# Hybrid trunk in FP32 parts: the first keys piece by half k, rotated 256-column pieces read in turn, boundary transposes in mid-unit

## The chip, the cores and the metric

One core of one Trainium2 chip runs the whole program. The metric is the time of one execution on the device in microseconds (us); the time before is a median of three runs.

## The reference

Two layers of a residual trunk over 256 tokens of width 1024. Each layer normalises the stream (RMS norm), multiplies it by one wide input matrix and feeds three parallel mixers: a Mamba-2 scan (A), sliding-window attention with rotated queries and keys (B) and forgetting attention (C). Their outputs are projected, gated, merged, projected once more and added to the stream; a last RMS norm ends it.

```python
for layer in range(DEPTH):
    h = rms_norm(x, norm_w[layer])
    proj = jnp.einsum('bsd,de->bse', h, w_in[layer])
    (a_xbc, a_z, a_dt, b_q, b_k, b_v, b_z, c_q, c_k, c_v, c_f, c_z, gates) = jnp.split(proj, split_at, axis=-1)
    y_a = mamba2_branch(a_xbc, a_z, a_dt, ...)
    y_b = sliding_window_branch(b_q, b_k, b_v, b_z, sinks[layer], cos, sin)   # rotates q and k
    y_c = forgetting_attention_branch(c_q, c_k, c_v, c_f, c_z, f_bias[layer])
    branch = jnp.einsum('bsiw,iwd->bsid', jnp.stack([y_a, y_b, y_c], axis=2), w_proj[layer])
    g = jax.nn.sigmoid(gates.reshape(b, s, N_BRANCH, d) + gate_bias[layer])
    x = x + jnp.einsum('bsd,de->bse', jnp.sum(g * branch, axis=2), w_out[layer])
return rms_norm(x, final_norm_w)
```

What matters here is the input product, the rotation (`rope`) of queries and keys, and the passage from one layer's output to the next layer's input.

## The kernel before

**Products.** The 256 tokens are two tiles of 128 (t = 0, 1), the width 1024 is eight steps k of 128 (`NK`). Every FP32 operand is split in two parts: a high part written by ScalarE in the matmul's format, and a low part, the difference, written by VectorE (`split`, line 255; the instructions carry lines 257 and 258). A product is three passes: high times high, low times high, high times low. `dense` (271) runs them for one tile and one weight piece k by k; `tok` (445) calls it with the tokens as the stationary operand and the weights moving. A unit is one piece for one tile: 24 matmuls.

**Weights.** A piece is 256 to 512 columns of a matrix. It is loaded on the SP queue in parts of up to 512 KB (`load_part`), six ahead (`N_RAW`), and split ahead as buffers come free (`feed`, `release`). A part of 256 columns holds four steps k.

**In turn.** With `turn` the moving operand is read in the order column 0, column n/2, column 1, and so on (`in_turn`, 237), and the result is put back in order where it leaves PSUM (`ordered`, 243). All pieces of 512 columns, the values piece of layer 0 and the pieces of the channel units are read so. Not so: the keys piece of layer 0, the queries 3 of both layers (256 columns) and the 272-column piece with the decay inputs and queries 0.

**Order.** `ops` (1067 to 1161) is a list of units by hand; TensorE takes them in that order. Work that hangs on a unit's result (transposes, attention, normalisation) waits in a list as a generator with a due time on a modelled TensorE clock (`launch`, with delays such as `D_H`), and `pump` puts what is due between units, or inside one where `tok` is given a `mid` (after the fourth k; by itself only for pieces of over 300 columns). `drain` forces it. The other engines' order follows from a scheduler, except in the opening, which is written out by hand.

**Opening (layer 0, lines 1193 to 1292).** x arrives in two loads for tile 0 and one for tile 1, among the first weight parts. `turn(t, j)` transposes half a tile on TensorE (four transposes) and multiplies by the norm weight on VectorE (1218); `high` (1222) and `low` (1226) split it; `w_high` (1230) and `w_low` (1234) split a weight part by halves, some of the lows on GpSimd (`gtt`). The row sums of squares come from `square` on ScalarE; the factor `y0.rn` is not yet known when the products run, so it multiplies their results later. The keys piece is the first: all passes of tile 0 with `second_rows` (the transposes of tile 1) behind its 16th and 20th matmul, then the splits of tile 1 (`first_end`), then tile 1. Its eviction waits in `late`. Then come the values piece, queries 1 and 2 (one piece of 512 columns), queries 3 (256), the 272-column piece, and `normalize`, which scales the transposed rows for everything after.

**Rotation.** `rope` (463) multiplies the result in PSUM by cosines and sines, three VectorE operations (472 without, 474 with the row factor), and GpSimd adds (498, 522).

**Boundary.** `out_end` (1003) adds the residual, takes the row factor of the finished stream, scales it (1037) and launches `hT` with `D_H[t]`, which transposes and splits a tile for the next layer. Layer 1 begins with keys and values tile 0, queries 3 tile 0, `drain(6)`, keys and values tile 1, queries 3 tile 1. `layer_consts` (400) loads a layer's small constants: for layer 0 on GpSimd's queue, for layer 1 on ScalarE's, listed late in layer 0.

Of the kernel before, what the change touches and what calls it, by code (L numbers as in the profile page):

```python
# [44 lines left out]
def hybrid_trunk(  # L45
# [149 lines left out]
        s.insert(axis, n)  # L195
        return ap.unsqueeze(axis).to_broadcast(s)

    def rsqrt(v, n):

        r0 = T("sm", [P, 8])  # L200
        nc.gpsimd.tensor_tensor(r0[:, :n], v[:, :n], mhalf[:, :n], op=ALU.pow)
        a = T("sm", [P, 8])
# [68 lines left out]
    def dense(pt, ah, al, bh, bl, w, after=None, mid=None):  # L271

        passes = ((ah, bh), (al, bh), (ah, bl))
        if after is None:
            seq = [(k, a, b) for k in range(NK) for a, b in passes]
        else:
            seq = [(k, a, b) for k0 in (0, 4) for a, b in passes for k in range(k0, k0 + 4)]
        for i, (k, a, b) in enumerate(seq):  # L280
            mm(pt, a(k), b(k), start=(i == 0), stop=(i == len(seq) - 1))
            if after is not None:
                after.get(i + 1, lambda: None)()
            elif i % 3 == 2:
                if w.last and (k + 1) % w.kper == 0:
                    release(w, k // w.kper + 1)
                if mid is not None and k == NK // 2 - 1:
                    mid()

    def dense2(ps_, as_, b, w, mids):  # L290

# [21 lines left out]
    late = []  # L313

    class Piece:
        def __init__(self, n):
# [128 lines left out]
    def tok(ah, al, w, t, turn=True, mid=None, bank=pmm, **kw):  # L445


        n = w.n
        p = bank()
        b = in_turn if turn else lambda ap: ap  # L450
        if mid is None and n > 300:
            mid = pump
        dense(p[:, 0:n], lambda k: ah[:, t, k, :], lambda k: al[:, t, k, :], lambda k: b(w.hi(k)),
              lambda k: b(w.lo(k)), w, mid=mid, **kw)
        return ordered(p[:, 0:n]) if turn else p[:, 0:n]

    def tok2(ah, al, w, mids):
# [4 lines left out]

    def rope(y, p, t):

        p4 = p.rearrange("p (h d) -> p h d", h=4)
        a = T("L1", [P, 4, 64])
        b = T("L1", [P, 4, 64])
        for o, i, r in ((a, p4, rope_sb[:, t, 0, :]),
                        (b[:, :, 0:32], p4[:, :, 32:64], rope_sb[:, t, 1, 0:32]),
                        (b[:, :, 32:64], p4[:, :, 0:32], rope_sb[:, t, 1, 32:64])):  # L470
            if y.rn is None:
                tt(o, i, bc(r, 1, 4), op=ALU.mult)
            else:
                stt(o, i, y.rn[:, t:t + 1], bc(r, 1, 4), op0=ALU.mult, op1=ALU.mult)
        return a, b

    def u_bkv(y, c0, t, after=None, end=lambda: None):

        def f(w):
            p = tok(y.hTh, y.hTl, w, t, turn=w.n == 512 or c0 > 0, after=after,  # L480
                    bank=pmx if after and t == 0 else pmm)
            end()
            if t == 0 and c0 == 0:
                kv = T("L8", [P, 2048])
                y.kT = kv[:, 0:1024].rearrange("p (h s) -> p h s", h=4)
                y.bv = kv[:, 1024:1536].rearrange("p (t c) -> p t c", t=2)
            (late.append if after is not None else lambda g: g())(lambda: evict(w, p))

        def evict(w, p):
            if c0 > 0:  # L490
                act(halves(y.bv[:, t, :]), p, AF.Copy, scale=y.rn[:, t:t + 1])
            elif w.n == 512:
                act(y.bv[:, t, :], p[:, 1, :], AF.Copy)
            if c0 == 0:
                a, b = rope(y, p if w.n == 256 else p[:, 0, :], t)
# [12 lines left out]
        return f  # L508

    def u_bq(y, c0, t):  # L510

        def f(w):
            p = tok(y.hTh, y.hTl, w, t, turn=w.n == 512)
            if w.n == 272:
                logits(y, t, 0, p[:, 0:16])
                p = p[:, 16:272]
            for i in range(w.n // 256):
                if t == 0:
                    y.qT[c0 + i] = T("qt", [P, 2, S])
                with tc.high_priority():  # L520
                    a, b = rope(y, p[:, i, :] if w.n == 512 else p, t)
# [545 lines left out]
    for y in layers:  # L1067
# [37 lines left out]

        if l == 0:
            k, v = cols(C_BK), cols(C_BV)
            op(k, u_bkv(y, 0, 0, {16: lambda: second_rows(0), 20: lambda: second_rows(1)}, lambda: first_end()))
            op(k, u_bkv(y, 0, 1, {}))
            op(v, u_bkv(y, 256, 0), u_bkv(y, 256, 1))  # L1110
# [82 lines left out]
    with tc.manual_schedule(engines={ENG.PE, ENG.DVE, ENG.Activation, ENG.Pool}):  # L1193
        load_to(2)
        nc.sync.dma_start(x0[:, 1, :], x2[P:S, :])
        nc.sync.dma_start(rope_sb, rope_tab.rearrange("(t p) c d -> p t c d", p=P))
        load_to(N_RAW)
        warm = pmx()
        for i in range(WARM):
# [29 lines left out]
            raw, hi, _ = part  # L1229
            act(hi[:, k:k + 2, :], raw[:, k:k + 2, :], AF.Copy)  # L1230

        def w_low(part, k, sub_=tt):
            raw, hi, lo = part
            sub_(lo[:, k:k + 2, :], raw[:, k:k + 2, :], hi[:, k:k + 2, :].bitcast(F32), op=ALU.subtract)

        def square(t, j):
            sum_sq(x0, t, 512 * j, ss[:, 2 * t + j:2 * t + j + 1], 512)

        parts = [new_part() for _ in range(4)]
        square(0, 0)  # L1240
        turn(0, 0)
        w_high(parts[0], 0)
# [15 lines left out]

        def second_rows(j):
            turn(1, j)  # L1260

        def first_end():
            high(1, 0)
            high(1, 1)
            low(1, 0)
            low(1, 1)
            w_high(parts[2], 0)
            w_high(parts[2], 2)
            w_low(parts[2], 2, gtt)
            w_low(parts[2], 0)  # L1270
            w_high(parts[3], 0)
            w_high(parts[3], 2)
            w_low(parts[3], 0)
            square(1, 0)
            square(1, 1)
            w_low(parts[3], 2)
            v = T("sm", [P, 8])
            nc.vector.tensor_reduce(v[:, 0:2], ss.rearrange("p (t j) -> p t j", t=2), axis=mybir.AxisListType.X,
                                    op=ALU.add)
            ts(v[:, 0:2], v[:, 0:2], 1.0 / D, EPS, op0=ALU.mult, op1=ALU.add)  # L1280
            y0.rn = rsqrt(v, 2)

        for i, f, _ in ops[:2]:
            f(pieces[i])
# [40 lines left out]
```

## Time and profile before

| | |
|---|---|
| runs without a profile | 841.45 us median, 841.16 to 841.69 |
| the profiled execution | 840.82 us, of it span 839.1 us |
| granted TensorE clock | 0.999 |
| TensorE busy | 830.2 us |
| VectorE, ScalarE, GpSimd busy | 650.0, 510.9, 108.1 us |
| loaded and stored | 157.85 MB, 188 GB/s in the mean |

The span runs from the first to the last instruction that the profile has; what lies around it (1.7 us) is not in any row. A row of the time line is start, length, engine, line, operation, result and sources with their sizes, count, and in brackets how long the engine was idle before and what ended that. PE is TensorE's matmuls, PEld its loads of the stationary operand, DVE VectorE, ACT ScalarE, POOL GpSimd, SP the queue of the loads; ACTq and POOLq are what those engines' sequencers do themselves. The matmul's recorded length includes its passage through the array, so the pace is read from start to start. In the chain of the work that ended last a piece is start, length and what it was; pieces with x24 are 24 matmuls in a row with nothing between. A row of the table of windows gives busy time and count of PE, PEld, DVE, ACT and POOL, the granted clock, the DMA engines' share and the GB/s moved.

### The profile page before, as it was taken

The numbers are of one execution on the slowest core, as the hardware profiler recorded it, in microseconds if no ns is written. First come the engines' busy times: TensorE is split into PE (matmuls) and PEld (weight loads), VectorE is DVE, ScalarE is ACT, GpSimd is POOL, SyncE is SP. The second block draws the span as 40 slices with busy tenths as digits, with TensorE's granted clock in tenths as the row PEclk, the third lists the DMA queues.
The fourth block names the chain that finished last, engine by engine and source line by source line (L and its number), as shares of the span: only waits on it lengthen the run. The fifth ranks groups of instructions, "written<-read, shape, count | busy, mean of one in ns | idle before, by whom it ended". The sixth has DMA issues, their size and how long they took to land.

```text
span 839.1 us, 16279 instructions
## 1 busy us (share of the span) xinstructions
PE 830.2 (99%) x6067; PEld 768.3 (92%) x6067; DVE 650.0 (77%) x1421; ACT 510.9 (61%) x1022; POOL 108.1 (13%) x144
## 2 busy tenths in 40 slices
PE   9999999999999999999999999999999999999996
PEld 8999999989999998888989999999899999988896
DVE  6897898998766679665777689899968667785665
ACT  7477768665666667353654676876557667654442
POOL 3810001000231010210024000100003110121000
PEclk9999999999999999999999999999999999999999
DMA  9755467666565556675676544766856564476622
GB/s 308 232 168 169 119 184 232 202 213 205 152 197 176 152 164 214 207 243 178 219 234 208 150 126 149 226 214 188 251 168 183 158 186 152 154 237 214 213 101 76
DMA packets 122841, 157.85 MB, mean 188 GB/s; under 512 B 5730, under 2 KB 89818, under 8 KB 122762
## 3 DMA queue, kind: packets, MB, share of 16 engines
q1 hardware_dynamic: 108816, 140.53, 53.4%
q10 hardware_dynamic: 13690, 16.24, 6.2%
q8 instruction: 48, 0.79, 0.4%
q14 instruction: 31, 0.25, 0.1%
q0 software_dynamic: 256, 0.05, 0.0%
HBM read 154.63 MB, written 2.16 MB: 187 GB/s over the span
## 4 chain that ended last, share of the span: by engine, by line
PE 99%; DVE 0%; ACT 0%; issue 0%; POOLq 0%; POOL 0%
PE mm L97 84%; PE mx L97 10%; PE mx L101 5%; DVE L L258 0%; DVE L L1218 0%; POOLq L1321 0%; ACT L L1031 0%; DVE L L1226 0%; ACT L L257 0%; DVE L L1006 0%; DVE L L1010 0%; POOL ident masks.py:199 0%; DVE sm L226 0%; POOL tri L168 0%; DVE sm L252 0%
## 5 line engine op out<-in xcount | busy, mean ns | idle before, releaser
L258 DVE TENSOR_TENSOR lo<-raw,hi 128x1024 fp32r<-128x1024 f32 (+3 forms) x262 | 310.6, 1199 | 89.6 <-ACT hi L257 81.6
L97 PE MATMUL mm<-hi,L 128*128 128x512 f32 (+4 forms) x1424 | 377.2, 352 | 0.7 <-ACT L L257 0.3
L257 ACT ACTIVATE hi<-raw 128x1024 fp32r<-128x1024 f32 (+3 forms) x262 | 264.1, 1022 | 90.1 <-PE mm L97 79.8
L97 PE MATMUL mm<-L,hi 128*128 128x256 f32 x1792 | 318.0, 278 | 0.0
L97 PEld LDWEIGHTS mm<-L,hi 128*128 128x128 f32 x1792 | 277.7, 192 | 7.4 <-issue 3.9
L97 PEld LDWEIGHTS mm<-hi,L 128*128 128x128 f32 x1424 | 251.0, 189 | 27.3 <-issue 2.1
L97 PE MATMUL mm<-lo,L 128*128 128x512 f32 (+4 forms) x712 | 247.2, 349 | 0.0
L97 PE MATMUL mm<-L,lo 128*128 128x256 f32 x896 | 246.4, 275 | 0.0
L97 PEld LDWEIGHTS mm<-L,lo 128*128 128x128 f32 x896 | 171.9, 192 | 0.2
L97 PEld LDWEIGHTS mm<-lo,L 128*128 128x128 f32 x712 | 134.3, 189 | 12.6 <-DVE lo L258 0.2
L877 POOL TENSOR_SCALAR_AFFINE_SELECT bias<-bias 128x128 f32<-128x128 f32 x64 | 35.8, 595 | 407.7 <-DMA bias<-cumd 211.8
L570 ACT ACTIVATE pp<-pp,nm 128x128 f32<-128x128 f32 (+1 forms) x128 | 56.6, 443 | 13.8 <-DVE nm L564 11.7
L699 DVE SCALAR_TENSOR_TENSOR L<-L,vec,L 128x255 f32<-128x255 f32 (+2 forms) x96 | 45.9, 479 | 2.1 <-ACT L L696 1.1
L702 ACT ACTIVATE L<-L 128x256 f32<-128x256 f32 x32 | 13.3, 417 | 41.1 <-DVE L L699 41.0
L97 PE MATMUL mx<-L,L 128*64 128x128 f32 (+1 forms) x384 | 34.4, 314 | 0.0
L901 ACT ACTIVATE L<-L 128x512 f32<-128x512 f32 x24 | 15.1, 630 | 31.1 <-DVE L L900 31.0
L582 DVE TENSOR_SCALAR pp<-pp,rsum 128x128 f32<-128x128 f32 (+1 forms) x128 | 32.3, 315 | 0.3
L97 PEld LDWEIGHTS mx<-L,L 128*64 128x64 f32 x384 | 23.0, 136 | 8.3 <-issue 1.4
L783 ACT ACTIVATE L<-mm 128x256 f32<-128x256 f32 x48 | 18.1, 378 | 20.2 <-PE mm L97 20.2
L599 ACT ACTIVATE L<-mx 128x512 f32<-128x512 f32 x48 | 26.8, 596 | 1.2 <-PE mx L101 1.0
L101 PE MATMUL mx<-ident,pp 128*128 128x128 f32 x192 | 26.3, 273 | 0.0
L900 DVE TENSOR_TENSOR L<-mm,L 128x512 f32<-128x512 f32 x24 | 16.4, 684 | 9.7 <-PE mm L97 9.7
(188 smaller groups left out, 731.8 us busy)
## 6 DMA issues: line engine op xcount, KB each, us to landing
raw<-in_w_in_dram SPq DMA_DIRECT2D x179, 512.0 KB, 4.4
raw<-in_w_proj_dram SPq DMA_DIRECT2D x48, 512.0 KB, 5.2
raw<-in_w_out_dram SPq DMA_DIRECT2D x16, 512.0 KB, 5.1
raw<-in_w_in_dram SPq DMA_DIRECT2D x16, 344.0 KB, 3.2
L<-cumd ACTq DMA_DIRECT2D x8, 512.0 KB, 4.7
bias<-cumd ACTq DMA_DIRECT2D x16, 256.0 KB, 3.4
L<-in_gate_bias_dram ACTq DMA_DIRECT2D x12, 256.0 KB, 6.3
raw<-in_w_in_dram SPq DMA_DIRECT2D x8, 352.0 KB, 3.1
```

What stands on the lines that cost most here:

```text
L97: nc.tensor.matmul(o, a, b, **kw)
L101: nc.tensor.transpose(o, a, i)
L257: keep(act)(hi, src, AF.Copy)
L258: keep(tt)(lo, src, hi.bitcast(F32), op=ALU.subtract)
L570: act(pp[:, i, sl], pp[:, i, sl], AF.Exp, scale=-1.0, bias=nm[:, e:e + 1], accum_out=sums[:, e:e + 1])
L582: ts(pp[:, i, sl], pp[:, i, sl], rs[:, 2 * i + b:2 * i + b + 1], 0.5, op0=ALU.mult, op1=ALU.mult)
L599: act(pT, pt, AF.Copy)
L699: stt(a[:, s:S], x_[:, 0:S - s], y.vec[:, 16 * j + u:16 * j + u + 1], a[:, s:S], op0=ALU.mult, op1=ALU.add)
L783: act(halves(th), p, AF.Tanh, scale=0.5)
L877: nc.gpsimd.affine_select(out=bias[:, i, dst], in_=bias[:, i, src], compare_op=ALU.is_ge, fill=NEG, base=0, pattern=[[-1, P]], channel_mul ...
L900: tt(halves(g), p, halves(y.gb), op=ALU.add)
L901: act(g, g, AF.Tanh, scale=0.5)
```

## The change

The keys piece of layer 0 is computed by half k for both tiles: a new function `keys` issues four matmuls, and the opening lists them by hand with the transposes of tile 1 between. All weight lows of the opening are on VectorE. The opening's end is written out in place of `second_rows` and `first_end`. The keys piece, and queries 3 in both layers, are read in turn (`turn=w.n != 272`). The rotation table is scaled once by layer 0's row factor, so `rope` has no factor any more, and the table is loaded again with layer 1's constants. Queries 3 of tile 0 in layer 1 has `pump` in its middle, and `D_H` of tile 1 is 6.4 instead of 7.0.

```diff
-D_GN1, D_GN2, D_CUM, D_H, D_M = 4.0, 6.0, 12.0, (4.8, 7.0), 5.0
+D_GN1, D_GN2, D_CUM, D_H, D_M = 4.0, 6.0, 12.0, (4.8, 6.4), 5.0
...
+    def load_rope(queue):
+        queue.dma_start(rope_sb, rope_tab.rearrange("(t p) c d -> p t c d", p=P))
...
         pdma = pin(queue.dma_start)
+        if l:
+            load_rope(queue)
...
-            if y.rn is None:
-                tt(o, i, bc(r, 1, 4), op=ALU.mult)
-            else:
-                stt(o, i, y.rn[:, t:t + 1], bc(r, 1, 4), op0=ALU.mult, op1=ALU.mult)
+            tt(o, i, bc(bc(r, 1, 2), 1, 2), op=ALU.mult)
...
-            p = tok(y.hTh, y.hTl, w, t, turn=w.n == 512 or c0 > 0, after=after,
-                    bank=pmx if after and t == 0 else pmm)
-            end()
+            p = tok(y.hTh, y.hTl, w, t) if placed is None else ordered(placed[t][:, 0:w.n])
...
-            p = tok(y.hTh, y.hTl, w, t, turn=w.n == 512)
+            p = tok(y.hTh, y.hTl, w, t, turn=w.n != 272, mid=mid)
...
-            op(q3, u_bq(y, 3, 0))
+            op(q3, u_bq(y, 3, 0, pump))
...
+        first.extend((pmx(), pmm()))
+
+        def keys(t, k0, a, b, ends=False):
+
+            for k in range(k0, k0 + 4):
+                mm(first[t][:, 0:256], a[:, t, k, :], in_turn(b(k)),
+                   start=(k == 0 and a is y0.hTh and not ends), stop=(k == NK - 1 and ends))
...
         low(0, 0)
         w_high(parts[0], 2)
+        high(0, 1)
         w_low(parts[0], 0)
-        w_low(parts[0], 2, gtt)
-        high(0, 1)
+        w_low(parts[0], 2)
         w_high(parts[1], 0)
+        w_high(parts[1], 2)
         low(0, 1)
+        hh(0, 0)
+        lh(0, 0)
+        hl(0, 0)
+        turn(1, 0)
+        hh(0, 4)
+        turn(1, 1)
+        lh(0, 4)
+        square(0, 1)
+        high(1, 0)
+        high(1, 1)
+        low(1, 0)
         w_low(parts[1], 0)
-        w_high(parts[1], 2)
-        w_low(parts[1], 2, gtt)
-        square(0, 1)
+        w_low(parts[1], 2)
+        low(1, 1)
+        hh(1, 0)
+        lh(1, 0)
+        hl(1, 0)
+        hl(0, 4)
+        hh(1, 4)
+        lh(1, 4)
+        hl(1, 4)
+        for k in (0, 2):
+            w_high(parts[2], k)
+            w_low(parts[2], k)
+        square(1, 0)
+        square(1, 1)
...
+        r0 = root(v, 2)
+        for k in (0, 2):
+            w_high(parts[3], k)
+            w_low(parts[3], k)
+        y0.rn = rsqrt(v, 2, r0)
+        for t in range(2):
+            ts(rope_sb[:, t, :, :], rope_sb[:, t, :, :], y0.rn[:, t:t + 1], None, op0=ALU.mult)
```

Here `hh(t, k0)`, `lh` and `hl` are `keys` with the high and low parts of the tokens and of the weights: high times high, low times high, high times low, for k0 to k0 + 3. `root` is the first step of `rsqrt`, taken out of it. In the changed kernel `dense` has lost its `after` branch.

More of the change, by code (lines that the diff above doesn't have):

```diff
@@ L196, in bc, with root, rsqrt @@
         return ap.unsqueeze(axis).to_broadcast(s)
-    def rsqrt(v, n):
+    def root(v, n):
         r0 = T("sm", [P, 8])
         nc.gpsimd.tensor_tensor(r0[:, :n], v[:, :n], mhalf[:, :n], op=ALU.pow)
+        return r0
+    def rsqrt(v, n, r0=None):
+        r0 = r0 or root(v, n)
         a = T("sm", [P, 8])
@@ L269, in to_hT, with dense @@
             split(hTh[:, t, 4 * j:4 * j + 4, :], hTl[:, t, 4 * j:4 * j + 4, :], pv)
[L271 to L277, printed above, removed]
-        else:
[L279 to L288, printed above, removed]
+    def dense(pt, ah, al, bh, bl, w, mid=None):
+        for k in range(NK):
+            for i, (a, b) in enumerate(((ah, bh), (al, bh), (ah, bl))):
+                mm(pt, a(k), b(k), start=(k == 0 and i == 0), stop=(k == NK - 1 and i == 2))
+            if w.last and (k + 1) % w.kper == 0:
+                release(w, k // w.kper + 1)
+            if mid is not None and k == NK // 2 - 1:
+                mid()
     def dense2(ps_, as_, b, w, mids):
@@ L312, in hybrid_trunk @@
     raws, pieces, pieces_out = {}, {}, {}
-    late = []
+    first, late = [], []
     class Piece:
@@ L443, in chan, with tok @@
         return ordered(p[:, 0:S])
-    def tok(ah, al, w, t, turn=True, mid=None, bank=pmm, **kw):
+    def tok(ah, al, w, t, turn=True, mid=None):
         n = w.n
-        p = bank()
+        p = pmm()
         b = in_turn if turn else lambda ap: ap
@@ L453, in tok @@
         dense(p[:, 0:n], lambda k: ah[:, t, k, :], lambda k: al[:, t, k, :], lambda k: b(w.hi(k)),
-              lambda k: b(w.lo(k)), w, mid=mid, **kw)
+              lambda k: b(w.lo(k)), w, mid=mid)
         return ordered(p[:, 0:n]) if turn else p[:, 0:n]
@@ L486, in f @@
                 y.bv = kv[:, 1024:1536].rearrange("p (t c) -> p t c", t=2)
-            (late.append if after is not None else lambda g: g())(lambda: evict(w, p))
+            (late.append if placed is not None else lambda g: g())(lambda: evict(w, p))
         def evict(w, p):
@@ L494, in evict @@
             if c0 == 0:
-                a, b = rope(y, p if w.n == 256 else p[:, 0, :], t)
+                a, b = rope(y, p if w.n == 256 else halves(p[:, 0, :]), t)
                 kd = T("L2", [P, 4, 2, 64])
@@ L508, in u_bkv, with u_bq @@
         return f
-    def u_bq(y, c0, t):
+    def u_bq(y, c0, t, mid=None):
         def f(w):
-            p = tok(y.hTh, y.hTl, w, t, turn=w.n == 512)
+            p = tok(y.hTh, y.hTl, w, t, turn=w.n != 272, mid=mid)
             if w.n == 272:
                 logits(y, t, 0, p[:, 0:16])
-                p = p[:, 16:272]
+                p = halves(p[:, 16:272])
             for i in range(w.n // 256):
@@ L520, in f @@
                 with tc.high_priority():
-                    a, b = rope(y, p[:, i, :] if w.n == 512 else p, t)
+                    a, b = rope(y, halves(p[:, i, :]) if w.n == 512 else p, t)
                     gtt(a, a, b, op=ALU.add)
@@ L1107, in hybrid_trunk @@
             k, v = cols(C_BK), cols(C_BV)
-            op(k, u_bkv(y, 0, 0, {16: lambda: second_rows(0), 20: lambda: second_rows(1)}, lambda: first_end()))
-            op(k, u_bkv(y, 0, 1, {}))
-            op(v, u_bkv(y, 256, 0), u_bkv(y, 256, 1))
+            op(k, *(u_bkv(y, 0, t, first) for t in range(2)))
+            op(v, *(u_bkv(y, 256, t) for t in range(2)))
             op(None, lambda: layer_consts(y0, nc.gpsimd))
@@ L1195, in hybrid_trunk @@
         nc.sync.dma_start(x0[:, 1, :], x2[P:S, :])
-        nc.sync.dma_start(rope_sb, rope_tab.rearrange("(t p) c d -> p t c d", p=P))
+        load_rope(nc.sync)
         load_to(N_RAW)
@@ L1230, in w_high, with w_low @@
             act(hi[:, k:k + 2, :], raw[:, k:k + 2, :], AF.Copy)
-        def w_low(part, k, sub_=tt):
+        def w_low(part, k):
             raw, hi, lo = part
-            sub_(lo[:, k:k + 2, :], raw[:, k:k + 2, :], hi[:, k:k + 2, :].bitcast(F32), op=ALU.subtract)
+            tt(lo[:, k:k + 2, :], raw[:, k:k + 2, :], hi[:, k:k + 2, :].bitcast(F32), op=ALU.subtract)
         def square(t, j):
@@ L1239, in hybrid_trunk, with hh, lh, hl @@
         parts = [new_part() for _ in range(4)]
+        first.extend((pmx(), pmm()))
[3 more added lines that the diff above has]
+                   start=(k == 0 and a is y0.hTh and not ends), stop=(k == NK - 1 and ends))
+        w0 = pieces[0]
+        def hh(t, k0):
+            keys(t, k0, y0.hTh, w0.hi)
+        def lh(t, k0):
+            keys(t, k0, y0.hTl, w0.hi)
+        def hl(t, k0):
+            keys(t, k0, y0.hTh, w0.lo, True)
         square(0, 0)
@@ L1248, in hybrid_trunk @@
         w_high(parts[0], 2)
+        high(0, 1)
         w_low(parts[0], 0)
-        w_low(parts[0], 2, gtt)
-        high(0, 1)
+        w_low(parts[0], 2)
         w_high(parts[1], 0)
+        w_high(parts[1], 2)
         low(0, 1)
-        w_low(parts[1], 0)
-        w_high(parts[1], 2)
-        w_low(parts[1], 2, gtt)
-        square(0, 1)
[L1259 to L1281, printed above, removed]
+        hh(0, 0)
[9 more added lines that the diff above has]
+        low(1, 0)
+        w_low(parts[1], 0)
+        w_low(parts[1], 2)
[12 more added lines that the diff above has]
+        square(1, 1)
+        v = T("sm", [P, 8])
+        nc.vector.tensor_reduce(v[:, 0:2], ss.rearrange("p (t j) -> p t j", t=2), axis=mybir.AxisListType.X,
+                                op=ALU.add)
+        ts(v[:, 0:2], v[:, 0:2], 1.0 / D, EPS, op0=ALU.mult, op1=ALU.add)
+        r0 = root(v, 2)
[5 more added lines that the diff above has]
+            ts(rope_sb[:, t, :, :], rope_sb[:, t, :, :], y0.rn[:, t:t + 1], None, op0=ALU.mult)
         for i, f, _ in ops[:2]:
```

12 lines of the change are left out of this document (6 added, 6 removed).

## The prediction

> **What bounds the kernel now.** I read the page first: its busy line, then the chain that ended last.
>
> ```profile
> PE 830.2 (99%) x6067; PEld 768.3 (92%) x6067; DVE 650.0 (77%) x1421; ACT 510.9 (61%) x1022; POOL 108.1 (13%) x144
> ...
> PE 99%; DVE 0%; ACT 0%; issue 0%; POOLq 0%; POOL 0%
> ```
>
> TensorE is the whole chain. So a microsecond counts only if it is taken from TensorE's stream: its own matmul pace, or one of its few waits. VectorE, ScalarE and GpSimd have room, and what they gain or lose counts only where TensorE stands behind them. Next I took the chain in order of time, where the diff touches it. Columns: start, length, what.
>
> ```profile
> 31.41 0.87 PE mx L101 x8
> 32.29 5.70 PE mm L97 x48
> ...
> 429.26 0.45 PE mx L101 x4
> ...
> 429.74 0.61 ACT L L257
> ...
> 430.37 0.70 DVE L L258
> ...
> 437.00 2.86 PE mm L97 x24
> ...
> 465.94 5.36 PE mm L97 x48
> ```
>
> Two things are to be seen. The rotated 256-column pieces that are read in plain order (queries 3 of layer 0 at 32.29, of layer 1 at 437.00) run at 5.70/48 = 0.119 us a matmul; 48 matmuls of 256 columns with an operand in turn (465.94) take 5.36, 0.112 each. And at the layer boundary the chain leaves TensorE: transposes, then ScalarE's high part, then VectorE's low part, before the keys-values unit of tile 1 can go on.
>
> **Queries in turn.** Four units of 24 matmuls (queries 3, two layers, two tiles) become 0.0071 us faster per matmul: 0.17 each, **-0.34** in layer 0 and -0.34 in layer 1. Against this stands a rule. The Trainium skill (Advanced Engine Details and Errata, section SBUF Cachelines) says that reads which keep to a 16-byte line run at full speed and a different line at each access costs. By it, reading in turn, which jumps 128 columns at every element, should be the dearer way and the sign of these terms would turn; the two rows above say the opposite here.
>
> **The boundary.** `mid=pump` and the shorter D_H put tile 1's eight transposes between the 12th and 13th matmul of the queries unit instead of behind it; the instruction order of the built kernel shows exactly that, and on VectorE the two splits ahead of the queries' rotation.
>
> ```profile
> 426.25 0.40 PE L97 MATMUL mm<-hi,L 128*128 128x256 f32 x2
> ...
> 426.45 1.41 DVE L1037 SCALAR_TENSOR_TENSOR L<-L,rs,nwb 128x512 f32<-128x512 f32 x2
> ...
> 428.33 0.38 ACT L493 ACTIVATE L<-mm 128x256 f32<-128x256 f32 x1 [4.57 <-DVE L L1037]
> 428.74 1.54 DVE L472 TENSOR_TENSOR L<-mm,rope 128x256 f32<-128x256 f32 x6 [0.88 <-ACT L L493]
> ...
> 431.65 0.59 PE L97 MATMUL mm<-hi,L 128*128 128x512 f32 x2
> ```
>
> From 426.25: 12 matmuls in turn, 1.34, to 427.59; eight transposes, 0.87 (row 31.41), to 428.46; 12 more to 429.80. The normalised rows they read come at 426.45 + 1.41 = 427.86; the first four transposes need only the first half, the other four start at 428.03, so 0.17 us in hand. ScalarE is free after 428.71 (it stands behind the load of the final weights, which waits for the same rows): highs at 429.3 and 429.9. VectorE rotates the keys first (half of 1.54, to 429.5), then the first low part, 0.70, to 430.2. The second matmul of the unit wants it at 430.02: a wait of about 0.2 is left. The next three matmuls then start at 430.63 instead of 431.65: **-1.02**, of which 0.17 is the pace. Tile 1's queries unit is the other **-0.17**. If the transposes moved but bought nothing, 0.85 of this stays away.
>
> **The start.** Now the rows of the first 16 us.
>
> ```profile
> 7.36 0.68 DVE L1234 TENSOR_TENSOR lo<-raw,hi 128x512 fp32r<-128x512 f32 x1
> 7.49 1.71 POOL L1234 TENSOR_TENSOR lo<-raw,hi 128x512 fp32r<-128x512 f32 x1 [4.37 <-ACT hi L1230]
> ...
> 7.79 1.20 PE L97 MATMUL mx<-hi,L 128*128 128x256 f32 x8
> 7.96 1.78 DVE L1226 TENSOR_TENSOR L<-L,L 128x512 fp32r<-128x512 f32 x1
> 8.48 1.15 ACT L1230 ACTIVATE hi<-raw 128x512 fp32r<-128x512 f32 x2 [0.55 <-DMA raw<-in_w_in_dram]
> ...
> 10.06 0.60 PE L101 MATMUL mx<-ident,L 128*128 128x128 f32 x4
> ...
> 10.70 0.69 DVE L1218 TENSOR_TENSOR L<-mx,L 128x512 f32<-128x512 f32 x1 [0.35 <-PE mx L101]
> 11.43 0.63 ACT L1222 ACTIVATE L<-L 128x512 fp32r<-128x512 f32 x1 [1.18 <-DVE L L1218]
> 12.11 1.58 PE L97 MATMUL mm<-hi,L 128*128 128x256 f32 x8
> 12.22 1.47 DVE L1226 TENSOR_TENSOR L<-L,L 128x512 fp32r<-128x512 f32 x2
> 12.95 0.53 PEld L97 LDWEIGHTS mm<-hi,L 128*128 128x128 f32 x4 [0.31 <-DVE L L1226]
> 13.53 0.64 PE L97 MATMUL mm<-lo,L 128*128 128x256 f32 x4
> ...
> 15.43 0.39 PE L97 MATMUL mm<-hi,L 128*128 128x256 f32 x2
> ...
> 23.81 0.19 PEld L97 LDWEIGHTS mm<-lo,L 128*128 128x128 f32 x1 [0.23 <-DVE lo L258]
> ```
>
> And one microsecond of the table of windows; its last column is GB/s moved.
>
> ```profile
> 9.00:10.00 1.00, 0.98 (x8) 0.77 (x8) 1.00 (x2) 1.00 (x3) 0.49 (x2) 1.00 1.05 361
> ```
>
> Before, the first values matmul is at 15.43. Two costs go: GpSimd's split (1.71) with the VectorE operation stretched beside it to 1.78 (the same shape at 7.36 takes 0.68). The new wait is the second tile's rows of x. The first 12 matmuls now end at 7.79 + 12 x 0.112 = 9.13, and TensorE then asks for those rows. They are loaded behind the weight part whose landing ScalarE awaited until 8.48; 524 KB more at 361 GB/s is 1.45 us, so about 9.93, and the first transpose at T = 10.0 (an estimate; 10.06 is the bound, where they ran before). Queued behind that transpose is everything TensorE has.
>
> From T the links are those of before: transposes to VectorE 0.64 (10.06 to 10.70), VectorE to ScalarE 0.73, ScalarE to matmul 0.68, VectorE to matmul 0.73 (12.22 to 12.95), VectorE back to back 0.60 (7.36 to 7.96). The second four transposes follow after four transposes and four matmuls, T + 0.88. VectorE multiplies them at T + 1.52, makes the first low part of tile 1 at T + 2.12, the two weight lows that GpSimd used to share at T + 2.72 and T + 3.32, the second low part at T + 3.92. TensorE needs the second weight low for two matmuls: T + 3.32 + 0.73 = T + 4.05. Behind it stand these two and 12 more, 14 x 0.112 = 1.56, plus 0.10 for a restart (12.95 to 13.53 is 0.58 for four at 0.119). First values matmul at T + 5.71 = 15.71 instead of 15.43: **+0.28**. VectorE, with more to do, has taken the place of GpSimd. Both ends: if nothing but TensorE counted, 36 matmuls and eight transposes after T are 4.02 + 0.87 = 4.89, so 14.89, -0.54; if VectorE's links were each 0.1 longer, +0.7.
>
> Do the values then find their weights? VectorE's next operations at its 0.60 pace, with the two small ones of the sum of squares, put the lows of the last two half parts at about 16.8 and 17.4; matmuls 15 and 21 want them at 17.3 and 18.0. Covered by half a microsecond. The values (48 matmuls in turn, 5.36) end at about 21.1 against 20.8; the wait at 23.81, of which 0.10 reaches TensorE's pace, goes, since the rotations ahead of that split on VectorE are shorter: **-0.10**.
>
> **Edits at nothing.** The rotation reads a table scaled once, so it loses the extra factor:
>
> ```profile
> 20.71 1.00 DVE L474 SCALAR_TENSOR_TENSOR L<-mx,rs,rope 128x256 f32<-128x256 f32 x3
> ...
> 438.89 0.81 DVE L472 TENSOR_TENSOR L<-mm,rope 128x256 f32<-128x256 f32 x3
> ...
> 46.68 0.69 ACT L1172 ACTIVATE L<-ident,rs 128x128 f32<-128x128 f32 x2
> 49.14 0.55 ACT L835 ACTIVATE L<-mm,rs 128x352 f32<-128x352 f32 x1 [1.77 <-PE mm L97]
> ...
> 50.52 0.63 ACT L257 ACTIVATE L<-L 128x512 fp32r<-128x512 f32 x1 [0.56 <-DVE L L1182]
> ...
> 53.26 0.31 PE L97 MATMUL mm<-lo,L 128*128 128x352 f32 x1
> ...
> 353.24 0.52 ACTq L252 DMA_DIRECT2D vr<-in_conv_w_dram  x1
> 353.79 0.60 ACTq L252 DMA_DIRECT2D vr<-in_conv_b_dram  x1
> 354.43 0.33 ACTq L252 DMA_DIRECT2D vr<-in_ssm_norm_w_dram  x1
> 354.80 0.36 ACTq L252 DMA_DIRECT2D nwb<-in_norm_w_dram  x1
> ...
> 358.96 2.00 ACT L257 ACTIVATE hi<-raw 128x1024 fp32r<-128x1024 f32 x2 [4.78 <-DMA nwb<-in_norm_w_dram]
> ```
>
> 0.19 saved per rotation and two scalings added, all on VectorE and hidden behind the weights that are split ahead. The table must be loaded again for layer 1, and the order shows a side effect: that load, and with it four of layer 1's constants, now stand on ScalarE's queue in layer 0, between the two operations of 46.68 and that of 49.14. Issuing the four costs 0.52 + 0.60 + 0.33 + 0.36 = 1.81 us and the table perhaps 0.45, their mean; ScalarE idled 1.77 there, so it is late by up to 0.5, for an evacuation that nobody awaits at once, and has 0.56 more to spare before the split of the normalised rows at 50.52. I take nothing; if that cover is gone, see the third rival.
>
> **Sum:** -0.34 - 1.02 - 0.17 + 0.28 - 0.10 = -1.35 on the profiled execution (span 839.1, own time 840.82): 839.5. The median of the runs is 841.45, 0.63 above it, so the forecast is **840.1 us** (839.6 to 840.6 by the bounds near it).
>
> **Rivals.** *The start gains:* the rows land earlier, or VectorE's links hide, so the floor of 4.89 holds: 0.82 less, 839.3. For it: VectorE and TensorE are nearly level in my chain. Against it: the rows' landing. *The boundary wait stays under another name* (the rows or the low part late in mid-unit): +0.85, 840.95. Only 0.17 us in hand speaks for it. *ScalarE's queue blocks:* at 353.24 the same loads held ScalarE until 358.96, 5.7 us, since a load also waits for an earlier one of its queue slot. If that happens at 47.1, ScalarE is free at 52.8 and, with two evacuations first, splits the rows from 53.6 instead of 50.52; the gate unit that follows the matmul of 53.26 at about 53.6 then waits for a high part, 0.63, another, and a low part, 0.68, some 1.7 us in all: 841.8, slower than before. Each further microsecond adds itself; it turns the sign from a block of about 5.4 us. Against it: the awaited weight load is issued several us earlier. *Reading in turn costs what it was to save:* 96 matmuls lose 0.0071 instead of gaining it, +1.36, 841.5; only the rows at 32.29 and 465.94 speak, and against it. The Trainium skill's rule of lines, above, would have it so.
>
> **Chances:** forecast 0.52, start gains 0.20, boundary wait 0.14, ScalarE's queue 0.10, reading in turn 0.04. The range is 839.0 to 841.6. About 0.2% (1.7 us) is what a measurement can tell from no change. Below 839.77: most of the start's gain and a sixth of the forecast's own case, 0.30. Above 843.13: a longer block of ScalarE, 0.06. Within: 0.64.
>
> **What would show it.** Right: 24 matmuls of queries 3 in 2.68 instead of 2.86; transposes at about 427.6 on the old time scale and the next triple one microsecond earlier; a gap on TensorE ended by the x load near 9.1 to 10.0, and waits on VectorE's splits before the values begin 0.3 later. Wrong: a values start below 15.2; a gap after the queries unit; any TensorE gap at 50 to 56 ended by ScalarE.

## Result and profile after

| | before | after |
|---|---|---|
| runs without a profile, same chip | 841.37 us median of 12 (840.94 to 843.99) | 839.45 us median of 12 (839.09 to 840.52) |
| profiled execution: own time, span | 840.82, 839.1 us | 839.45, 837.7 us |

The ratio is 0.9976 with a 95% interval of 0.9967 to 0.9985: 1.92 us less, where the forecast had 1.35 less. The profiled executions differ by 1.37 us (spans by 1.4), as the sum said (840.82 - 1.35 = 839.5). So the steps held, and what failed is the last addition, from the profiled execution to the median. The interval of the ratio is 1.3 to 2.8 us: the medians alone don't exclude the 1.35.

The page of after, busy line and chain:

```profile
PE 828.7 (99%) x6067; PEld 767.2 (92%) x6067; DVE 650.2 (78%) x1426; ACT 510.9 (61%) x1022; POOL 102.3 (12%) x141
...
PE 98%; DMA 1%; DVE 0%; SPq 0%; POOLq 0%; issue 0%; ACT 0%
```

TensorE is still the bound; the new 1% is the load of x in the opening. The chain in order of time, at the places shown of before:

```profile
31.62 0.87 PE mx L101 x8
32.49 5.36 PE mm L97 x48
...
435.87 2.68 PE mm L97 x24
```

Queries 3 take 5.36 and 2.68 instead of 5.70 and 2.86. At the boundary the chain no longer leaves TensorE. The time line of the opening and of the boundary shows how:

```profile
9.94 0.66 PE L101 MATMUL mx<-ident,L 128*128 128x128 f32 x4 [0.54 <-DMA L<-in_x_dram]
...
12.73 1.29 DVE L1230 TENSOR_TENSOR lo<-raw,hi 128x512 fp32r<-128x512 f32 x2
...
12.86 0.52 PEld L97 LDWEIGHTS mm<-hi,L 128*128 128x128 f32 x4 [0.30 <-DVE L L1222]
...
13.93 0.68 DVE L1222 TENSOR_TENSOR L<-L,L 128x512 fp32r<-128x512 f32 x1
...
15.73 0.39 PE L97 MATMUL mm<-hi,L 128*128 128x256 f32 x2
...
45.99 0.42 ACTq L396 DMA_DIRECT2D rope<-in_rope_dram  x1
...
49.01 0.55 ACT L832 ACTIVATE L<-mm,rs 128x352 f32<-128x352 f32 x1 [1.76 <-PE mm L97]
...
420.94 0.60 PE L97 MATMUL mm<-hi,L 128*128 128x512 f32 x2
...
426.12 0.38 PE L97 MATMUL mm<-hi,L 128*128 128x256 f32 x2
...
427.46 1.04 PE L101 MATMUL mx<-ident,L 128*128 128x128 f32 x8
...
429.67 0.80 PE L97 MATMUL mm<-hi,L 128*128 128x512 f32 x2
...
430.52 0.60 PE L97 MATMUL mm<-hi,L 128*128 128x512 f32 x2
```

TensorE waits for the rows of x until 9.94 and for the first low part of tile 1 until 12.86, and the first values matmul comes at 15.73. From the first matmul of queries 3 (426.12) to the second triple of the next unit (430.52) it is 4.40 us; before, 426.25 to 431.65, it was 5.40. The constants that moved to ScalarE's queue are issued from 45.99 on, and ScalarE then still waits 1.76 for TensorE: they cost nothing.

### The profile page after: what moved, and what is told of

It reads as the page before. It is cut to its first block, busy times and chain, and to the rows that moved or that the text cites. A ratio compares the mean times of both kernels' runs of the same rounds, so it can differ in the third digit from the quotient of the medians.

```text
span 837.7 us, 16280 instructions
## 1 busy us (share of the span) xinstructions
PE 828.7 (99%) x6067; PEld 767.2 (92%) x6067; DVE 650.2 (78%) x1426; ACT 510.9 (61%) x1022; POOL 102.3 (12%) x141
## 4 chain that ended last, share of the span: by engine, by line
PE 98%; DMA 1%; DVE 0%; SPq 0%; POOLq 0%; issue 0%; ACT 0%
PE mm L97 84%; PE mx L97 9%; PE mx L101 4%; DMA L<-in_x_dram 1%; SPq L330 0%; SPq L164 0%; DVE L L1214 0%; POOLq L1346 0%; ACT L L1028 0%; DVE L L1222 0%; DVE L L1003 0%; DVE L L1007 0%; DVE sm L230 0%; DVE rs L232 0%; DVE sm L256 0%
## 5 line engine op out<-in xcount | busy, mean ns | idle before, releaser
L874 POOL TENSOR_SCALAR_AFFINE_SELECT bias<-bias 128x128 f32<-128x128 f32 x64 | 34.1, 569 | 409.5 <-DMA bias<-cumd 291.1
L898 ACT ACTIVATE L<-L 128x512 f32<-128x512 f32 x24 | 15.2, 631 | 36.5 <-DVE L L897 36.3
```

The source lines that it names most:

```text
L874: nc.gpsimd.affine_select(out=bias[:, i, dst], in_=bias[:, i, src], compare_op=ALU.is_ge, fill=NEG, base=0, pattern=[[-1, P]], channel_mul ...
L898: act(g, g, AF.Tanh, scale=0.5)
```

## Experiments

Each kernel is the changed one with one edit, except where it says otherwise. Times are medians without a profile; ratios are to the kernel before on the same chip (841.6 to 841.83 there), where after has 0.9976, and 0.997 when it was run again (run 7). Executions of one of these kernels spread over 0.5 to 1.8 us, those of before over up to 3.2, so differences of some tenths are read from the traces.

**1. Queries 3 in plain order again.**

```diff
-            p = tok(y.hTh, y.hTl, w, t, turn=w.n != 272, mid=mid)
+            p = tok(y.hTh, y.hTl, w, t, turn=w.n == 512, mid=mid)
```

> The changed kernel with queries 3 read in plain order again (both layers); all else stays, the keys piece of layer 0 included. If the pace is a matter of the reading order alone, queries 3 of layer 0 take 5.70 us again instead of 5.36 and those of layer 1 2.86 instead of 2.68 each, and the span grows by 0.68 us, from 837.7 to about 838.4. Rival: the pace came from something else in the change (the lighter VectorE, other neighbours); then they stay near 5.36 and 2.68 and the span stays at 837.7.

Measured: 839.66 us, ratio 0.997 (0.996 to 0.9981), span 838.2 (+0.5). The two chains have the same pieces, with these lengths here:

```profile
32.47 5.64 PE mm L97 x48
...
436.15 2.86 PE mm L97 x24
```

0.28 and 0.18 come back in the units shown (0.34 and 0.18 expected). The reading order sets the pace; which property of it, runs 2 and 3 ask.

**2. Nine orders in one run (gate units, 512 columns).** The first kernel reads a groups of 512/a columns, one element of each in turn (each group is called a stream below); the second reads pairs, i columns apart.

```diff
+            mix = lambda ap: ap.rearrange("p (a i) -> p i a", a=a)
...
+            mix = lambda ap: ap if i == 1 else ap.rearrange("p (b a i) -> p b i a", a=2, i=i)
```

> The changed kernel with its gate units (512 columns) read in nine orders: a groups of 512/a columns, one element of each in turn, with a = 1 (plain), 2 (the order of the kernel), 4, 8, 16, 32, 64, 128, 256. Theory (the plain order alone is slow): a = 1 takes about 2 x 0.119 = 0.238 us a matmul, all others about 0.224, whatever the jump. Rival 1 (the rule of lines of 16 bytes): plain is the fastest, the jumps of 4 columns and more are alike and dearer, and the jump of 2 columns (a = 256) lies between. Rival 2 (a bank pattern): the pace varies with the jump, with a = 2 among the fast.

> The changed kernel with its gate units (512 columns) read in pairs: blocks of 2i columns, in each of them column 0, column i, column 1, column i + 1 and so on, with i = 256 (the order of the kernel), 128, 64, 32, 16, 8, 4, 2, and 1 (plain). In the run before, two groups took 0.216 us a matmul, plain order 0.235, four groups (jumps of 128 columns) 0.283 and eight or more 0.43 to 0.49. Theory (what counts is that two streams alternate, not how far they lie apart): all i from 2 to 256 take 0.21 to 0.22. Rival 1 (the jump counts: short ones are dear): 0.216 for 256 and 128, rising to 0.4 and more at 64 and below. Rival 2 (the rule of lines of 16 bytes): i = 2 costs no more than plain, since both columns lie in one line, and all others are dearer than it.

The pace is read from the start of one triple of matmuls to that of the next. First kernel: L279 is plain, L281 two groups, L283 four, L285 eight.

```profile
146.00 0.63 PE L279 MATMUL mm<-hi,L 128*128 128x512 f32 x2
...
146.70 0.63 PE L279 MATMUL mm<-hi,L 128*128 128x512 f32 x2
...
148.04 0.59 PE L281 MATMUL mm<-hi,L 128*128 128x512 f32 x2
...
148.69 0.59 PE L281 MATMUL mm<-hi,L 128*128 128x512 f32 x2
...
177.57 0.73 PE L283 MATMUL mm<-hi,L 128*128 128x512 f32 x2
...
178.42 0.73 PE L283 MATMUL mm<-hi,L 128*128 128x512 f32 x2
...
185.86 1.19 PE L285 MATMUL mm<-hi,L 128*128 128x512 f32 x2
...
187.34 1.18 PE L285 MATMUL mm<-hi,L 128*128 128x512 f32 x2
```

Second kernel: L281 is i = 2, L283 is i = 4.

```profile
150.75 0.63 PE L281 MATMUL mm<-hi,L 128*128 128x512 f32 x2
...
151.46 0.63 PE L281 MATMUL mm<-hi,L 128*128 128x512 f32 x2
...
178.37 0.59 PE L283 MATMUL mm<-hi,L 128*128 128x512 f32 x2
...
179.02 0.59 PE L283 MATMUL mm<-hi,L 128*128 128x512 f32 x2
```

A triple takes 0.70 plain, 0.65 in two groups, 0.85 in four, 1.48 in eight, and 1.29 to 1.38 in 16 to 256. Of the pairs, i = 2 takes 0.71, as plain; i = 4 takes 0.65, and so do all up to 256. So my expectation of the first kernel ("all others fast") fell, and that of the second fell at i = 2: of the orders tried, fast is the alternation of two streams that lie at least 4 columns, 16 bytes, apart. The Trainium skill (Advanced Engine Details and Errata, section SBUF Cachelines) puts a line at 16 bytes and says that a different line at each access costs. The step between i = 2 and i = 4 lies at just that size, but has the other sign: two alternating lines are 7% faster than staying in one. From four streams on the rule's sign holds (+21%, then about double). Each order was profiled once, and three streams weren't tried. What inside the chip makes two streams the best is not shown.

**3. The 272-column piece in turn, as 34 groups of 8 and as 2 groups of 136.**

```diff
+                mix = lambda ap: ap.rearrange("p (a i) -> p i a", a=34)
...
+                q = T("L2", [P, 512])[:, 0:272]
+                act(q.rearrange("p (a i) -> p a i", a=2), p, AF.Copy)
```

> The changed kernel with the 272-column piece read in turn too, as 34 groups of 8 columns (each element jumps 8 columns). Theory (any order other than one column after the next is the faster one): the 96 matmuls of these units go from 0.1253 to 272 times 0.112/256 = 0.119 us, -0.6 us in all, 838.8. Rival 1 (only jumps of half the piece are fast): no change, 839.3 to 839.6. Rival 2 (the rule of lines, 8 columns being 32 bytes): slower per matmul, 0.13 and more, +0.5 us or more.

Measured: 849.92 us, ratio 1.0095 (1.008 to 1.0111). A loss of 10 us where I expected 0.6 less; the unit of tile 1 in layer 0, of this kernel and of after, in the chain:

```profile
44.20 5.57 PE mm L97 x24
```

```profile
41.95 3.01 PE mm L97 x24
```

That is 0.232 a matmul instead of 0.125: the factor of the many-group orders above, and four units of 2.56 are the 10 us.

> The changed kernel with its 272-column piece read in turn as two groups of 136; one more ScalarE operation per unit copies the result out of PSUM in order. Theory (two groups are the fast order at any width): 24 matmuls go from 3.0 to about 2.85 us, four units, -0.6 us: 0.6 below the changed kernel on the same chip. Rival (the 0.006 a matmul is lost on the way, the copy delaying the first attention of the piece or ScalarE's splits): within 0.2 of the changed kernel, and no gap of TensorE shorter than before.

Measured: 838.83 us, ratio 0.9966 (0.9952 to 0.9979). The pieces of layer 1, of this kernel and of after:

```profile
438.86 5.76 PE mm L97 x48
```

```profile
439.01 6.23 PE mm L97 x48
```

The pace gains 0.47 per layer, more than expected, yet the median is only 0.27 below that of after on the same chip (run 7), within the intervals. In this trace 0.4 is given back at the boundary: from the first triple of keys and values tile 0 (420.94 in after) to the second of tile 1 (430.52) it is 9.98 us, against 9.58 in after. Another 0.27 goes at 235.66, where TensorE waits for VectorE (L768) and in after doesn't; the second kernel of run 7 shows the same wait.

**4. No transposes in mid-unit.**

```diff
-            op(q3, u_bq(y, 3, 0, pump))
+            op(q3, u_bq(y, 3, 0))
...
-D_GN1, D_GN2, D_CUM, D_H, D_M = 4.0, 6.0, 12.0, (4.8, 6.4), 5.0
+D_GN1, D_GN2, D_CUM, D_H, D_M = 4.0, 6.0, 12.0, (4.8, 7.0), 5.0
```

> The changed kernel without the pump in the middle of the queries unit, with tile 1's delay at 7.0 again. If the boundary's gain is the transposes' place, the eight transposes stand behind the unit, TensorE waits again for ScalarE's high part and VectorE's low part (about 1.0 us), the next triple of the keys-values unit starts 0.85 to 1.0 us later, and the span is about 838.6. Rival: the wait went because VectorE splits before it rotates the queries, whose order is not forced here; then the gap stays below 0.4 us and the span near 837.9.

Measured: 840.86 us, ratio 0.9986 (0.9977 to 0.9995), span 839.3 (+1.6). The time line of TensorE:

```profile
426.71 0.38 PE L97 MATMUL mm<-hi,L 128*128 128x256 f32 x2
...
430.67 0.48 PE L97 MATMUL mm<-hi,L 128*128 128x512 f32 x1 [0.25 <-ACT L L261]
...
431.51 0.48 PE L97 MATMUL mm<-hi,L 128*128 128x512 f32 x1 [0.35 <-DVE L L262]
...
432.04 0.59 PE L97 MATMUL mm<-hi,L 128*128 128x512 f32 x2
```

Both waits of before are back, and the stretch is 432.04 - 426.71 = 5.33 instead of 4.40: 0.93, with the pace in turn in both. The other 0.6 arose ahead of this stretch: 0.46 of it at tile 0, between 417.5 and 426.7 (run 7). The rest is chance: this opening was 0.37 earlier than that of after, and a wait at 162.17 cost 0.44.

**5. The old opening, with GpSimd's splits and without, and the kernel before once more.** The first has everything of after but the opening, whose lines are those that the diff of the change removes; the second takes GpSimd out of it; the third is the kernel before, unedited.

```diff
-        w_low(parts[0], 2, gtt)
+        w_low(parts[0], 2)
...
-        w_low(parts[1], 2, gtt)
+        w_low(parts[1], 2)
...
-            w_low(parts[2], 2, gtt)
+            w_low(parts[2], 2)
```

> The changed kernel with the opening of the kernel before: keys piece tile by tile and read in plain order, GpSimd's three splits, the transposes of tile 1 after the 16th and 20th matmul; the rotation table is scaled at the end of it. By the forecast's terms the new opening costs 0.28 less 0.10: the first values matmul is at about 15.43 instead of 15.73, layer 0's queries 3 begin about 0.2 earlier than 32.49, and the span is about 837.5. Rival: the new opening gains something that the trace's first 32 us do not show (the runs' medians differ by 1.9, my terms by 1.35); then this kernel is slower than the changed one, by about 0.5 us or more.

> The kernel before, profiled a second time. Theory (the old opening has two outcomes, by whether VectorE or GpSimd takes the first of two weight lows that start within 0.1 us of each other): either VectorE's first weight low takes 0.68 us again and the first values matmul is at 15.4, or it takes about 1.8 us and the values start at 15.9 to 16.1, with a span of about 839.6. Rival (nothing of the kind; the profiled execution was short for another reason): VectorE's first low takes 0.68 and the values start within 0.1 of 15.43 again.

> The changed kernel with the opening of before, as in the earlier run, but all weight lows of that opening on VectorE. Theory (GpSimd's splits beside VectorE's are what the old opening loses): no low of 128x512 takes over 0.75 us, the first values matmul comes at 15.2 to 15.6 instead of 16.03, median 0.4 to 0.9 below the 840.37 of the old opening, that is 839.5 to 840.0. Rival (the order of the passes costs, all of tile 0 before the transposes of tile 1): VectorE, with two more operations in the chain, starts the values at 16.0 or later and the median stays within 0.2 of 840.37.

Old opening: 840.37 us, ratio 0.9981 (0.9972 to 0.999), span 838.8; I had expected it below after, and it is above. On the same chip even run 1, with the slower queries, has 839.66. Its time line:

```profile
7.41 1.29 POOL L1241 TENSOR_TENSOR lo<-raw,hi 128x512 fp32r<-128x512 f32 x1 [4.28 <-ACT hi L1237]
7.44 1.80 DVE L1241 TENSOR_TENSOR lo<-raw,hi 128x512 fp32r<-128x512 f32 x1
...
9.24 1.74 POOL L1241 TENSOR_TENSOR lo<-raw,hi 128x512 fp32r<-128x512 f32 x1 [0.55 <-ACT hi L1237]
...
9.77 1.77 DVE L1241 TENSOR_TENSOR lo<-raw,hi 128x512 fp32r<-128x512 f32 x1
...
16.03 0.27 PE L97 MATMUL mm<-hi,L 128*128 128x256 f32 x1
```

GpSimd began 0.03 us ahead of VectorE, took its 1.29, and VectorE, whose split takes 0.68 alone, ended 0.54 after it. In the profile of before VectorE began 0.13 ahead: it took 0.68, GpSimd 1.71, and the next VectorE operation paid. The second pair makes the difference between the two. In before VectorE was 0.04 ahead (9.67 against 9.71), and its next operation, on the transposes in PSUM, took its usual 0.69 at 10.70. Here GpSimd was ahead again, VectorE took 1.77, and the same operation began at 11.46. The second profile of before (841.21 us, span 839.5):

```profile
8.06 1.51 POOL L1234 TENSOR_TENSOR lo<-raw,hi 128x512 fp32r<-128x512 f32 x1 [4.94 <-ACT hi L1230]
8.53 1.59 DVE L1226 TENSOR_TENSOR L<-L,L 128x512 fp32r<-128x512 f32 x1
...
15.81 0.39 PE L97 MATMUL mm<-hi,L 128*128 128x256 f32 x2
```

Here a weight part landed later, and the values start 0.38 later than in the first. In all three the stretched VectorE operation ends 0.54 to 0.55 us after GpSimd does. That fits the Trainium skill (SBUF — State Buffer, section Who interferes with whom), by which a VectorE instruction with two SBUF inputs contends with a GpSimd instruction that reads SBUF, the shared ports are locked exclusively, and the order of issue decides which one blocks. Without GpSimd's splits:

```profile
7.30 1.28 DVE L1241 TENSOR_TENSOR lo<-raw,hi 128x512 fp32r<-128x512 f32 x2
...
15.00 0.38 PE L97 MATMUL mm<-hi,L 128*128 128x256 f32 x2
```

No split is stretched and the values start at 15.00, 0.4 to 1.0 ahead of the three above: the theory's side, though VectorE does more. Part of it is the draw: the transposes of tile 1 start at 9.65 here, and the values come 5.35 after them (5.37 in before, 5.79 in after). With rows as late as the 10.03 of the latest profile that would be about 15.4, an estimate. The median is 839.92, ratio 0.9979 (0.997 to 0.9988): by the ratios no measurable difference to the old opening, and the half-k order of the change is not needed for this start. Where the lead goes, run 6 shows.

**6. Weight lows ahead of the second tile.** The lows of the second weight part while TensorE waits for x, the keys' remaining weight pass of tile 0 before tile 1.

```diff
         hl(0, 0)
+        w_low(parts[1], 0)
+        w_low(parts[1], 2)
...
+        hl(0, 4)
```

> The changed kernel with its opening in another order: VectorE makes the two weight lows of the second half part while TensorE waits for the x rows (it idles then from 9.5 to 10.6), TensorE runs the low-weight pass of tile 0's second half ahead of tile 1's, and the weight lows of the last half parts come before the sums of squares. If VectorE's chain behind the x rows is what took GpSimd's place, TensorE runs after the rows with two short waits at most, the first values matmul is at about 14.9 (the floor of the forecast) instead of 15.73, and the span falls by 0.5 to 0.8, to about 837.0. Rival: the x rows and TensorE's own work bind, not VectorE's order; then the first values matmul stays at 15.5 to 15.7 and the span at 837.6.

Measured: 839.94 us, ratio 0.9978 (0.9969 to 0.9987), span 838.0 instead of about 837.0. The edit also moves the weight lows of the values ahead of the sums of squares and puts `root` back into `rsqrt`. The values start as expected, and the lead is lost before 25.5:

```profile
14.91 0.28 PE L97 MATMUL mm<-hi,L 128*128 128x256 f32 x1
...
23.75 0.48 PE L97 MATMUL mm<-lo,L 128*128 128x512 f32 x1 [0.29 <-DVE lo L262]
...
25.42 0.48 PE L97 MATMUL mm<-lo,L 128*128 128x512 f32 x1
```

VectorE of this kernel, and below it of after, shows the bound:

```profile
17.51 0.16 DVE L207 TENSOR_TENSOR sm<-sm 128x2 f32<-128x2 f32 x1 [0.90 <-POOL sm L200]
...
18.70 2.35 DVE L262 TENSOR_TENSOR lo<-raw,hi 128x1024 fp32r<-128x1024 f32 x2
```

```profile
18.48 2.35 DVE L262 TENSOR_TENSOR lo<-raw,hi 128x1024 fp32r<-128x1024 f32 x2
```

VectorE stands 0.90 for a step of the row factor on GpSimd, a gap that after fills with the weight lows of the values. So it begins the lows of queries 1 and 2 at 18.70, against 18.48 in after and 18.50 with the opening of run 5 that starts the values at 15.00. At 23.75 and 25.42 TensorE waits for the third and the fourth of them. The chain names another bound ahead of these lows, a weight load that lands at 20.99. By the order of ScalarE's splits that is the first part of queries 3: the four parts of queries 1 and 2 were split by 20.4. With the two groups of run 3 this part was split later still (21.27 against 21.10) and TensorE didn't wait; there VectorE had begun the lows at 18.03. TensorE starts queries 3 at 32.61, against 32.49 in after (32.41 with that opening of run 5): the earlier values bought nothing. First transpose at 9.96, values at 14.91, is 4.95 apart; my floor was 4.89.

**7. The changed kernel again, and residual rows loaded earlier.** The second kernel is that of run 3 with two groups, and loads the residual rows of the last out pieces one unit or more ahead.

```diff
+            ahead[y.l, t] = {256: out_start(y, 256, t, 1, 512), 768: out_start(y, 768, t, 2, 256)}
```

> The changed kernel once more, for the spread of its opening and for a comparison with the other kernel of this call on the same chip. Expected: median 839.3 to 839.7; first values matmul between 15.2 and 15.8, by when the rows of x land (first transpose at 9.5 to 10.0); in five openings of this form so far it was 15.26 to 15.73, in three of the old form 15.43 to 16.03. Rival (the old form is the steadier one): values at 15.9 or later.

> The 272-column piece read as two groups, and besides it the residual rows of the last two out pieces are loaded one unit to several units earlier. In one profile of the changed kernel the first of them landed 1.9 us late (VectorE waited 1.6 for it) and TensorE lost 0.9 between 421 and 431 us. Theory (the boundary's leftover is this load): no wait of VectorE for these rows, the three matmuls after tile 0's transposes start without a gap, span 836.6 to 837.2, median 838.4 to 838.8. Rival (the late rows were one case in six, or the two extra buffers held from the ring delay others): median 838.8 or more, and any gap at 420 to 432 comes from something else.

The repeat: 839.1 us (838.6 to 840.42), a little below what I expected, ratio 0.997 (0.9959 to 0.998), 2.73 us below before on that chip; its profiled execution is the slowest of the seven, span 838.7, one microsecond above the first profile of the same kernel. The time line shows where most of it goes:

```profile
411.66 0.69 DVE L1003 TENSOR_TENSOR L<-mm,L 128x512 f32<-128x512 f32 x1 [1.61 <-DMA L<-in_x_dram]
...
421.83 0.48 PE L97 MATMUL mm<-hi,L 128*128 128x512 f32 x1 [0.41 <-DVE sm L221]
```

The opening is 0.07 later than in after (values at 15.80). At 411.66 VectorE waits for residual rows (409.73 in after); its queue runs a microsecond late from there, and TensorE waits at 421.83 and again near 431: the stretch defined in run 3 is 10.46 us instead of 9.58. The "other 0.6" of run 4 sits at the same place, with a smaller wait (0.2) of the same name. With the rows loaded earlier:

```profile
409.47 0.69 DVE L1015 TENSOR_TENSOR L<-mm,L 128x512 f32<-128x512 f32 x1 [0.22 <-PE mm L97]
...
420.69 0.60 PE L97 MATMUL mm<-hi,L 128*128 128x512 f32 x2
...
430.26 0.59 PE L97 MATMUL mm<-hi,L 128*128 128x512 f32 x2
```

VectorE waits for TensorE alone there, and the stretch is 9.57. Median 838.76, ratio 0.9963 (0.995 to 0.9977): the lowest of all, at the edge of what I expected, and not to be told from two groups alone (838.83). Of the two, the pace is shown in the trace; the gain of the earlier load is one profile against one.

## Why the prediction was right, and where it was off

- **Queries in turn, -0.34 and -0.17:** right. 5.70 became 5.36 and 2.86 became 2.68; run 1 gives them back. The reason, as I told it against the rule of lines, was too simple: run 2 shows that only two streams gain.
- **Boundary, -1.02:** right. The stretch went from 5.40 to 4.40. Even the wait of 0.2 that I left is there: the first triple takes 430.52 - 429.67 = 0.85 instead of 0.65. Run 4 brings the waits back for 0.93.
- **Start, +0.28:** right for the profiled pair. T was 9.94 (forecast 10.0), the values came 5.79 after it (forecast 5.71), at 15.73 against 15.43. The route is only half the one I counted. VectorE's operations at 12.73 and 13.93 stand in the order counted, but the second weight low ended at 14.01, just as TensorE came to its matmul (14.08). What TensorE lost are the waits until 12.04 and 12.86 for the first high and low part of tile 1; 24 matmuls follow, nearly without a gap. Both routes give the same start within about 0.1, so the size was partly luck. Run 6, with other matmuls in these waits, starts the values 0.82 earlier. Nine profiles with this opening have T between 9.47 and 10.03, and values 5.79 or 5.80 after T in each.
- **Wait at 23.81, -0.10:** right. From the first values matmul to the transposes ahead of queries 3 it was 15.98 and is 15.89 (31.41 and 31.62 in the chains).
- **Edits at nothing:** right; ScalarE's queue didn't block.
- **From the profiled execution to the median, +0.63:** this step failed. I took the distance of before's median from its profile as a property of the program and added it to the forecast. After's profile lies on its median (839.45 and 839.45), which is nearer to the time of my first rival (839.3) than to my 840.1; but that rival's mechanism, the floor of 4.89 with values below 15.2, is in none of the nine profiles. The runs show what differs between executions of one kernel: the landing of x (T over 0.56 us in nine profiles, and seven of them waited for it), which of VectorE and GpSimd takes the ports first (old opening alone), and the residual rows (up to 0.9). In the time lines the transposes ahead of queries 3 start at 31.25, 31.64 and 32.27 with the old opening and GpSimd's splits, mean 31.72, and at 30.99 to 31.55, mean 31.28, in the nine with the new one. So over draws the start gains about 0.4, where the first pair, which I forecast, showed a loss of 0.2; the difference of 0.6 is the size of what was missing (1.92 against 1.35). A late opening is not made good later: the old opening's profile, 0.81 behind after at these transposes (32.27 and 31.46), is 0.82 behind at the transposes of tile 0 at the boundary (418.21 and 417.39). With three profiles against nine, and 2.73 us instead of 1.92 when after was run again, this is a fitting account and not proof; why runs without a profile of before lie 0.2 to 1.0 above both its profiled ones in their medians stays open.

## What to carry to other kernels

A profile is one draw: before a row becomes a term, ask what decided it in that execution (a load's landing, which of two engines came first), and do not carry the distance between one profile and the median over to another kernel. A lead in one stage is worth what the next split chain lets through; look for that bound before counting it. The cause that a chain names for a wait is inferred: check by the order of the operations which part it was. Splits given to GpSimd beside VectorE's own can cost VectorE more than doing them itself.

## What the runs showed of the hardware

- Reading the moving operand as two alternating streams at least 16 bytes apart takes 0.216 us per 512 columns, one column after the next 0.235, four streams 0.283, eight 0.49, and 16 to 256 streams 0.43 to 0.46.
- A VectorE subtraction of 0.68 us beside a GpSimd one took 1.59 to 1.80 and ended 0.54 to 0.56 us after it; where the two began within 0.13 us of each other, the first (by 0.03 to 0.13) kept its time and the other was stretched, GpSimd from 1.29 to 1.71 and 1.79.
- TensorE began on the rows of x for tile 1 over a span of 0.56 us in nine profiles, in seven of them after a wait for their load, and VectorE got one load of residual rows 1.9 us later in one execution of the kernel than in another.
